# Reordering the entry of an eight-core diffusion trunk: load order, split modulation, squares summed on TensorE, a chunked first matmul group

## The chip, the cores and the metric

The kernel runs on all eight cores of one Trainium2 chip, each with its own share of the tokens and the whole set of weights. The metric is the device time of the slowest core in microseconds (us). Some executions fall into a slower state, in which the cores of one die show a lower granted clock; only executions of the fast state are compared here.

## The reference, cut to what matters

Two trunk layers work on tokens of width 1024. Each sub-layer norms its input and modulates it with a scale and a shift that come from a small product of the condition vector; each layer is two half-step SwiGLU FFNs around a mixer.

```python
def modulate(x, g, shift, scale):
    return rms_norm(x, g) * (1 + scale[:, None, :]) + shift[:, None, :]

def swiglu(h, w1, w2):
    gate, up = jnp.split(h @ w1, 2, axis=-1)
    return (jax.nn.silu(gate) * up) @ w2

for l in range(DEPTH):
    mod = jax.nn.silu(cvec) @ ada_w[l] + ada_b[l]  # (Bc, 9D)
    sh1, sc1, g1, sh2, sc2, g2, sh3, sc3, g3 = jnp.split(mod, N_MOD, axis=-1)
    x = x + 0.5 * g1[:, None, :] * swiglu(modulate(x, norm_g[l, 0], sh1, sc1),
                                          ffn_w1[l, 0], ffn_w2[l, 0])
    # ... mixer (attention and convolution in layer 0, pooling in layer 1), second FFN
```

So before the first FFN matmul a core needs: x of a tile, its sum of squares, the scale and shift of the first FFN (a quarter of a layer's `ada_w` less a bit: 8 of 36 blocks), and a block of `w1`.

## The kernel before: the parts that the change touches

A core has 1280 tokens in three tiles (512, 512, 256 columns), held transposed: 128 partitions, 8 chunks of the model width. Weights come through a ring of 16 slots; one load reads 1 MiB of float32 and lands as bf16 (the cast is GpSimd's queue's). The program is planned in Python while it is built: generators yield operations, a list scheduler gives each a start time from a small cost model, takes the earliest, and so fixes the order of every engine's instructions. **On the chip each engine follows that order, whatever really lands first** (run 2 shows it: norm steps whose inputs are ready at 67 us run at 96). The DMA model serves all loads one after another in the order of issue, at `DMA_RATE` bytes per ns.

```python
# ... Sched
    DMA_RATE = 330.0
    DMA_LAT = 1900.0
# ... xload: all of x on SyncE's queue, tile after tile, in halves
        for t, (c0, n, v) in enumerate(TILES):
            for hf in range(2):
                # ...
                yield self.dma(SP, self.xres[:, 4 * hf:4 * hf + 4, c0:c0 + n], src, [], ...)
# ... order of the ring loads (GpSimd's queue)
            yield from ada(0, 0, 8)                       # shift blocks 0-3, scale blocks 4-7
            yield from mix(w1(0, 0), ada(0, 8, 36))
            yield from w2(0, 0)
            # ... mixer weights
            yield from mix(w1(0, 1), ada(1, 0, 20))
# ... rstd: one float32 matmul with ones over the summed squares
        acc = yield from self.sumsq(t, ver, engs)         # ScalarE/GpSimd square, VectorE/GpSimd add
        yield self.mm([(ps, self.onesf[:], acc[1][:, 0:n], True, True)], ..., f32=True)
# ... norm
        yield self.wait(("asc", l, i))                    # all four scale blocks (the shifts came earlier)
        for c in range(8):
            yield self.stt(nv, self.xres[:, c, c0:c0 + n], asc[:, i, c, v:v + 1], r, ALU.mult, ALU.mult, ...)
            # ... then ScalarE adds the shift and writes hbuf[:, c]
# ... ffn: a tile is taken only when all 8 chunks of h are planned
                if j >= NJ or not self.has(("h", t, l, i), 8) or ("w1", l, s, j) not in self.W:
                    continue
```

## Time and profile before

| | before |
|---|---|
| median of 5 executions | 1657.51 us (fast ones 1654.14 to 1657.51) |
| spans of the cores, profiled execution | 1638.5 to 1652.5 us |
| TensorE busy | 88% of the span |
| first FFN matmul (mean of the eight cores) | 112.5 us |
| first FFN over, that is first product of the mixer (mean) | 369.6 us |
| mixer over, that is first matmul of the second FFN (mean) | 705.0 us |

The three stage times are read from each core's TensorE timeline: they split the span into entry, first FFN, mixer and rest. The lines themselves are in the prediction. A line of a timeline has start and duration in us, engine, line of kernel.py, operation, output<-input, shapes and count; in brackets follow the engine's idle time before it and what ended that. A line of the chain of waits has start, duration and what the kernel waited for or did. h is the normed and modulated input of an FFN (`hbuf`); a ring load is named after its weights (`adaw` for a modulation block, `w1t` for a block of w1).

### The profile page before, as it was taken

The numbers are of one execution on the slowest core, as the hardware profiler recorded it, in microseconds if no ns is written. First come the engines' busy times: TensorE is split into PE (matmuls) and PEld (weight loads), VectorE is DVE, ScalarE is ACT, GpSimd is POOL, SyncE is SP. The second block draws the span as 40 slices with busy tenths as digits, with TensorE's granted clock in tenths as the row PEclk, the third lists the DMA queues.
The fourth block names the chain that finished last, engine by engine and source line by source line (L and its number), as shares of the span: only waits on it lengthen the run. The fifth ranks groups of instructions, "written<-read, shape, count | busy, mean of one in ns | idle before, by whom it ended". The sixth has DMA issues, their size and how long they took to land.

```text
span 1652.5 us, 25909 instructions; the slowest of 8 cores (1638.5 to 1652.5 us)
## 1 busy us (share of the span) xinstructions
PE 1453.5 (88%) x9548; PEld 804.2 (49%) x9548; DVE 515.9 (31%) x936; ACT 428.6 (26%) x690; POOL 368.3 (22%) x479
## 2 busy tenths in 40 slices
PE   0039999999888786889999999999999869999997
PEld 0015555545654443445555456555544635555445
DVE  0142222135775122442222134222213574222133
ACT  1141111111303767541111014111101264111000
POOL 3111110144622010111000444110035530000244
PEclk9999999999999575799999999999999979999999
DMA  9969996300479300077434106994312273331012
GB/s 175 194 96 143 154 150 116 52 7 11 71 131 153 65 2 1 1 119 130 75 61 77 26 1 94 169 176 75 63 26 40 48 132 65 64 62 29 1 51 77
DMA packets 43068, 131.48 MB, mean 80 GB/s; under 512 B 6336, under 2 KB 10176, under 8 KB 42944
## 3 DMA queue, kind: packets, MB, share of 16 engines
q0 software_dynamic: 33440, 117.27, 43.3%
q1 hardware_dynamic: 9504, 12.54, 2.7%
q8 instruction: 79, 1.29, 0.3%
q14 instruction: 45, 0.37, 0.1%
HBM read 240.50 MB, written 6.55 MB: 150 GB/s over the span
## 4 chain that ended last, share of the span: by engine, by line
PE 74%; DMA 8%; DVE 5%; ACT 5%; issue 4%; POOL 2%; another core or an unknown queue 2%; DVEq 0%; SPq 0%; ACTq 0%; POOLq 0%
PE ps L291 74%; DMA sb_ring<-adaw 5%; DMA sb_xres<-xin 3%; DVE sb_nt L310 2%; ACT sb_sg L307 1%; ACT sb_hbuf L307 1%; ACT sb_areg L307 1%; DVE sb_areg L315 1%; POOL sb_ring L340 1%; DVE sb_xres L310 1%; DVE sb_sg L315 1%; ACT sb_rs L307 0%; DVE sb_acc L315 0%; POOL sb_acc L315 0%
## 5 line engine op out<-in xcount | busy, mean ns | idle before, releaser
L291 PE MATMUL ps<-sb_hbuf,sb_ring 128*128 128x512 bf16 (+1 forms) x4512 | 835.3, 346 | 18.6 <-ACT sb_hbuf L307 15.4
L291 PEld LDWEIGHTS ps<-sb_hbuf,sb_ring 128*128 128x128 bf16 x4512 | 438.7, 98 | 387.6 <-issue 34.3
L291 PE MATMUL ps<-sb_areg,sb_ring 128*128 128x512 bf16 (+1 forms) x2304 | 425.8, 346 | 5.0 <-DVE sb_xres L310 4.2
L315 DVE TENSOR_TENSOR sb_areg<-ps,sb_sg 128x512 bf16<-128x512 f32 (+1 forms) x264 | 159.0, 602 | 546.3 <-PE ps L291 541.1
L291 PEld LDWEIGHTS ps<-sb_areg,sb_ring 128*128 128x128 bf16 x2304 | 224.9, 98 | 201.0 <-issue 17.5
L307 ACT ACTIVATE sb_sg<-ps 128x512 f32<-128x512 f32 (+3 forms) x280 | 146.8, 525 | 660.4 <-PE ps L291 644.8
L315 POOL TENSOR_TENSOR sb_sq<-sb_xres 128x512 f32<-128x512 f32 (+1 forms) x102 | 98.3, 965 | 381.9 <-DVE sb_xres L310 222.7
L310 DVE SCALAR_TENSOR_TENSOR sb_xres<-ps,sb_gsc,sb_xres 128x512 f32<-128x512 f32 (+1 forms) x144 | 93.2, 658 | 253.0 <-PE ps L291 248.9
L315 POOL TENSOR_TENSOR sb_acc<-sb_acc,sb_sq 128x512 f32<-128x512 f32 (+1 forms) x102 | 115.8, 1136 | 17.9 <-DVE sb_acc L315 3.8
L340 POOL DMA_DIRECT2D sb_ring<-w1t x88 | 47.8, 547 | 288.1 <-PE ps L291 251.4
L310 DVE SCALAR_TENSOR_TENSOR sb_nt<-sb_xres,sb_asc,sb_rs 128x512 f32<-128x512 f32 (+1 forms) x144 | 99.1, 721 | 39.5 <-ACT sb_rs L307 24.0
L291 PE MATMUL ps<-sb_acc,sb_onesf 128*128 128x512 f32 (+1 forms) x42 | 23.4, 644 | 96.0 <-DVE sb_acc L315 53.5
L291 PE MATMUL ps<-sb_areg 64*128 64x512 bf16 (+3 forms) x728 | 87.7, 315 | 17.0 <-ACT sb_areg L307 9.1
L307 ACT ACTIVATE sb_hbuf<-sb_nt,sb_modsb 128x512 bf16<-128x512 f32 (+1 forms) x144 | 89.8, 649 | 39.6 <-DVE sb_nt L310 38.8
L340 POOL DMA_DIRECT2D sb_ring<-w2t x44 | 23.3, 529 | 271.6 <-PE ps L291 264.6
L307 ACT ACTIVATE sb_rs<-ps 128x512 f32<-128x512 f32 (+1 forms) x21 | 11.0, 524 | 263.8 <-PE ps L291 263.6
L340 POOL DMA_DIRECT2D sb_ring<-adaw x72 | 39.3, 548 | 165.8 <-PE ps L291 156.9
L307 ACT ACTIVATE sb_areg<-ps,sb_amask 128x1024 bf16<-128x1024 f32 x48 | 52.6, 1114 | 46.8 <-PE ps L291 46.6
L291 PEld LDWEIGHTS ps<-sb_areg 64*128 64x128 bf16 (+1 forms) x728 | 39.4, 109 | 49.6 <-issue 41.3
L291 PE MATMUL ps<-sb_scb,sb_ring 128*128 128x2 bf16 x1152 | 38.8, 164 | 25.5 <-DMA sb_ring<-adaw 25.5
L291 PEld LDWEIGHTS ps<-sb_scb,sb_ring 128*128 128x128 bf16 x1152 | 38.0, 98 | 44.3 <-issue 35.2
L307 ACT ACTIVATE sb_sg<-ps,sb_amask 128x1024 bf16<-128x1024 f32 x48 | 53.2, 1115 | 11.7 <-PE ps L291 11.0
(66 smaller groups left out, 459.9 us busy)
## 6 DMA issues: line engine op xcount, KB each, us to landing
sb_ring<-w1t POOLq DMA_DIRECT2D x88, 512.0 KB, 9.8
sb_ring<-adaw POOLq DMA_DIRECT2D x72, 512.0 KB, 10.7
sb_ring<-w2t POOLq DMA_DIRECT2D x44, 512.0 KB, 6.2
sb_xres<-xin SPq DMA_DIRECT2D x4, 1024.0 KB, 39.1
sb_areg<-mp POOLq DMA_DIRECT2D x5, 512.0 KB, 7.0
sb_ring<-wcx POOLq DMA_DIRECT2D x4, 512.0 KB, 10.8
sb_ring<-wo POOLq DMA_DIRECT2D x4, 512.0 KB, 26.7
yo<-sb_nt SPq DMA_DIRECT2D x8, 256.0 KB, 2.1
```

The lines of the kernel that those rows point to most:

```text
L291: ins = e.matmul(m[0], lhsT=m[1], rhs=m[2], start=m[3], stop=m[4], **({"skip_group_check": True} if len(m) > 5 else {}))
L307: return Op(ACT, lambda e: e.activation(out=out, in_=in_, func=func, **kw), reads, writes, cost)
L310: return Op(DVE, lambda e: e.scalar_tensor_tensor(out=out, in0=in0, scalar=scalar, in1=in1, op0=op0, op1=op1), reads, writes, 150.0 + 1.04 ...
L315: return Op(eng, lambda e: e.tensor_tensor(out=out, in0=in0, in1=in1, op=op), reads, writes, c)
L340: return Op(q, lambda e: e.dma_start(out=out, in_=in_), reads, writes, 600.0 if q == POOL else 450.0, True, nbytes, key)
```

## The change

Its intent is to let TensorE start on the first FFN as soon as one tile is there, by asking for less before it.

```diff
-    DMA_RATE = 330.0
+    DMA_RATE = 315.0
 # xload: SyncE's queue brings tile 0 only
+        yield from self.xtile(0, SP)
+        yield self.wait("xin")
 # order of the ring loads
-            yield from ada(0, 0, 8)
-            yield from mix(w1(0, 0), ada(0, 8, 36))
+            for i in range(4):
+                yield from ada(0, 4 + i, 5 + i)
+                yield from ada(0, i, i + 1)
+            a = list(w1(0, 0))
+            yield from a[0:6]
+            yield from mix(a[6:], ada(0, 8, 28))
 ...
+            yield from ada(0, 28, 36)                     # after the mixer's weights
             yield from mix(w1(0, 1), ada(1, 0, 20))
+            if key in (("w1", 0, 0, 2), ("w1", 0, 0, 3)): # tiles 1 and 2 of x on GpSimd's queue
+                yield from self.xtile(key[3] - 1, POOL)
+                self.sigl("xin")
 # norm: two chunks wait for their own scale and shift block
-        yield self.wait(("asc", l, i))
         for c in range(8):
+            yield self.wait(("mod", l, i, c // 2), 2)
 # entry norm: bf16 squares, summed by eight bf16 matmuls with ones
+        IN = [(ACT, True), (DVE, True)] * 4
         for t in range(3):
-            S.spawn(self.norm(t, 1, 0, 0, MX), 0)
+            S.spawn(self.norm(t, 1, 0, 0, IN), 0)
 # first group of the first FFN: w1 blocks 0 and 1, chunk by chunk over four PSUM banks
+            if (l, s) == (0, 0) and j == 0 and ("w1", l, s, 1) in self.W:
+                # ...
+                for c in range(8):
+                    yield self.wait(("h", t, l, i), c + 1)
+                    yield self.mm([(self.psv(ks[q], n), ..., self.hbuf[:, c, c0:c0 + n], c == 0, c == 7)
+                                   for q in range(4)], ...)
 # dependencies: an engine now also waits for its own earlier reads of what it overwrites
-            for x in b.r:
-                if x.eng == eng and not x.is_dma and not dma and eng != POOL and not x.strict:
-                    continue
-                deps.add(x)
+            deps.update(b.r)
```

More of the change, by code (lines that the diff above doesn't have):

```diff
@@ L48 @@
     __slots__ = ("eng", "fn", "reads", "writes", "cost", "is_dma", "nbytes", "key", "deps", "marked", "sig", "dval",
-                 "t_end", "strict")
+                 "t_end")
     def __init__(self, eng, fn, reads, writes, cost, is_dma=False, nbytes=0, key=None):
@@ L55, in __init__ @@
         self.marked = False
-        self.strict = False
         self.sig = 0
@@ L454, in build @@
         self.identb = self.sb("identb", [128, 128], BF16)
+        self.onesb = self.sb("onesb", [128, 128], BF16)
+        self.b_onesb = Buf("onesb")
         self.cvec = self.sb("cvec", [128, 8, 2])
@@ L475, in build @@
              "dummy")]
-        self.b_mod = [[B("mod%d_%d" % (l, i)) for i in range(9)] for l in range(2)]
-        self.b_asc = [[B("asc%d_%d" % (l, i)) for i in range(3)] for l in range(2)]
+        self.b_mod = [[[B("mod%d_%d_%d" % (l, i, q)) for q in range(4)] for i in range(9)] for l in range(2)]
+        self.b_asc = [[[B("asc%d_%d_%d" % (l, i, q)) for q in range(4)] for i in range(3)] for l in range(2)]
         self.b_gsc = [[B("gsc%d_%d" % (l, i)) for i in range(3)] for l in range(2)]
@@ L502, in setup @@
         S.commit(self.memset(self.onesf[:], 1.0, [self.b_onesf]))
+        S.commit(self.memset(self.onesb[:], 1.0, [self.b_onesb]))
         S.commit(self.memset(self.dummy[:], 1.0, [self.b_dummy]))
@@ L508, in setup, with xtile @@
         S.commit(self.act(self.scb[:], self.cvec[:], AF.Silu, [self.b_cvec], [self.b_scb]))
-    def xload(self):
-        off = 0
-        for t, (c0, n, v) in enumerate(TILES):
-            for hf in range(2):
-                src = self.d_x[:, off:off + 4 * n].rearrange("p (c n) -> p c n", n=n)
-                off += 4 * n
-                yield self.dma(SP, self.xres[:, 4 * hf:4 * hf + 4, c0:c0 + n], src, [],
-                               [self.bx[t][4 * hf + i] for i in range(4)], 128 * 4 * n * 4, key="x%d%d" % (t, hf))
-                for i in range(4):
-                    self.sigl(("x", t, 4 * hf + i))
+    def xtile(self, t, q):
+        c0, n, v = TILES[t]
+        off = 8 * c0
+        for hf in range(2):
+            src = self.d_x[:, off:off + 4 * n].rearrange("p (c n) -> p c n", n=n)
+            off += 4 * n
+            yield self.dma(q, self.xres[:, 4 * hf:4 * hf + 4, c0:c0 + n], src, [],
+                           [self.bx[t][4 * hf + i] for i in range(4)], 128 * 4 * n * 4, key="x%d%d" % (t, hf))
+            for i in range(4):
+                self.sigl(("x", t, 4 * hf + i))
+    def xload(self):
+        yield from self.xtile(0, SP)
+        yield self.wait("xin")
         for (tl, d, b, nb) in ((self.finalg, self.d_finalg, self.b_finalg, 4096),
@@ L568, in seq @@
         def seq():
-            yield from ada(0, 0, 8)
-            yield from mix(w1(0, 0), ada(0, 8, 36))
+            for i in range(4):
+                yield from ada(0, 4 + i, 5 + i)
[3 more added lines that the diff above has]
+            yield from mix(a[6:], ada(0, 8, 28))
             yield from w2(0, 0)
@@ L602, in ada @@
         for l in range(2):
-            for s in range(36):
+            for s in ((4, 0, 5, 1, 6, 2, 7, 3) if l == 0 else tuple(range(8))) + tuple(range(8, 36)):
                 key = ("ada", l, s)
@@ L616, in ada @@
                 i = part // 3
-                bm = self.b_mod[l][part]
+                bm = self.b_mod[l][part][s % 4]
                 yield self.tt(self.modsb[l][:, m0:m0 + 2, :], ps,
@@ L621, in ada @@
                 self.unbank(k)
-                if s % 4 == 3:
-                    lo = 8 * part
-                    if part % 3 == 0:
-                        self.sigl(("shift", l, i))
-                    elif part % 3 == 1:
-                        a = self.asc[l][:, i, :, :]
-                        ba = self.b_asc[l][i]
-                        yield self.ts(a, self.modsb[l][:, lo:lo + 8, :], 1.0, None, ALU.add, None, [bm], [ba])
-                        yield self.tt(a, a, self.normg[:, l, i, :].unsqueeze(2).broadcast_to([128, 8, 2]), ALU.mult,
-                                      [ba, self.b_normg], [ba])
-                        self.sigl(("asc", l, i))
-                    else:
-                        g = self.gsc[l][:, i, :, :]
-                        bg = self.b_gsc[l][i]
-                        if i == 1 and l == 1:
-                            yield self.tt(g, self.modsb[l][:, lo:lo + 8, :],
-                                          self.pscale[:, :].unsqueeze(2).broadcast_to([128, 8, 2]), ALU.mult,
-                                          [bm, self.b_pscale], [bg])
-                        else:
-                            yield self.ts(g, self.modsb[l][:, lo:lo + 8, :], 1.0 if i == 1 else 0.5, None, ALU.mult,
-                                          None, [bm], [bg])
-                        self.sigl(("gate", l, i))
@@ new lines, in ada @@
+                lo = m0 % 8
+                if part % 3 == 0:
+                    self.sigl(("mod", l, i, s % 4))
+                elif part % 3 == 1:
+                    a = self.asc[l][:, i, lo:lo + 2, :]
+                    ba = self.b_asc[l][i][s % 4]
+                    yield self.ts(a, self.modsb[l][:, m0:m0 + 2, :], 1.0, None, ALU.add, None, [bm], [ba])
+                    yield self.tt(a, a, self.normg[:, l, i, lo:lo + 2].unsqueeze(2).broadcast_to([128, 2, 2]), ALU.mult,
+                                  [ba, self.b_normg], [ba])
+                    self.sigl(("mod", l, i, s % 4))
+                elif s % 4 == 3:
+                    lo = 8 * part
+                    g = self.gsc[l][:, i, :, :]
+                    bg = self.b_gsc[l][i]
+                    bms = self.b_mod[l][part]
+                    if i == 1 and l == 1:
+                        yield self.tt(g, self.modsb[l][:, lo:lo + 8, :],
+                                      self.pscale[:, :].unsqueeze(2).broadcast_to([128, 8, 2]), ALU.mult,
+                                      bms + [self.b_pscale], [bg])
+                    else:
+                        yield self.ts(g, self.modsb[l][:, lo:lo + 8, :], 1.0 if i == 1 else 0.5, None, ALU.mult,
+                                      None, bms, [bg])
+                    self.sigl(("gate", l, i))
@@ L650, in prefetch, with rstd @@
                         [self.b_dummy], 1500.0)], 0)
-    def sumsq(self, t, ver, engs):
+    def rstd(self, t, ver, plan):
         c0, n, v = TILES[t]
-        acc = yield from self.take(self.accp)
-        ba, a = acc[0], acc[1][:, 0:n]
-        for d in range(8):
-            yield self.wait(("x", t, d), ver)
-            x = self.xres[:, d, c0:c0 + n]
-            bxx = self.bx[t][d]
-            e = engs[d]
-            if d == 0:
-                if e == POOL:
-                    yield self.tt(a, x, x, ALU.mult, [bxx], [ba], POOL)
-                else:
-                    yield self.act(a, x, AF.Square, [bxx], [ba])
-                continue
-            sq = yield from self.take(self.sqp)
-            bs, s = sq[0], sq[1][:, 0:n]
-            def tail(e=e, x=x, bxx=bxx, bs=bs, s=s, sq=sq, d=d):
-                if e == POOL:
-                    yield self.tt(s, x, x, ALU.mult, [bxx], [bs], POOL)
-                    yield self.tt(a, a, s, ALU.add, [ba, bs], [ba], POOL)
-                else:
-                    yield self.act(s, x, AF.Square, [bxx], [bs])
-                    yield self.tt(a, a, s, ALU.add, [ba, bs], [ba], DVE)
-                self.sqp.give(sq)
-                self.sigl(("sumd", t, ver))
-            self.S.spawn(tail(), 1)
-        yield self.wait(("sumd", t, ver), 7)
-        return acc
@@ L684, in rstd, with squares, one @@
-    def rstd(self, t, ver, engs):
-        c0, n, v = TILES[t]
-        acc = yield from self.sumsq(t, ver, engs)
-        k = yield from self.bank()
+        acc = None
+        if not all(pe for e, pe in plan):
+            acc = yield from self.take(self.accp)
+        done, got = ("sumd", t, ver), {}
+        def squares():
+            first = True
+            for d in range(8):
+                e, pe = plan[d]
+                yield self.wait(("x", t, d), ver)
+                x, bxx = self.xres[:, d, c0:c0 + n], self.bx[t][d]
+                if first and not pe:
+                    first = False
+                    yield self.square(e, acc[1][:, 0:n], x, bxx, acc[0])
+                    self.sigl(done)
+                    continue
+                sq = yield from self.take(self.sqp)
+                def one(e=e, pe=pe, x=x, bxx=bxx, sq=sq, d=d):
+                    s = sq[1].bitcast(BF16)[:, 0:n] if pe else sq[1][:, 0:n]
+                    yield self.square(e, s, x, bxx, sq[0])
+                    if pe:
+                        got[d] = sq
+                    else:
+                        a = acc[1][:, 0:n]
+                        yield self.tt(a, a, s, ALU.add, [acc[0], sq[0]], [acc[0]], POOL if e == POOL else DVE)
+                        self.sqp.give(sq)
+                        self.sigl(done)
+                self.S.spawn(one(), 1)
@@ new lines, in rstd @@
+        self.S.spawn(squares(), 0)
+        parts = ([] if acc is None else [None]) + [d for d in range(8) if plan[d][1]]
+        nacc = sum(1 for e, pe in plan if not pe)
+        k = None
+        for q, d in enumerate(parts):
+            if d is None:
+                yield self.wait(done, nacc)
+                src = acc
+            else:
+                yield Wait(lambda d=d: d in got)
+                src = got[d]
+            if k is None:
+                k = yield from self.bank()
+            lo = d is not None
+            rhs = src[1].bitcast(BF16)[:, 0:n] if lo else src[1][:, 0:n]
+            yield self.mm([(self.psv(k, n), self.onesb[:] if lo else self.onesf[:], rhs, q == 0, q == len(parts) - 1)],
+                          [src[0], self.b_onesb if lo else self.b_onesf], [self.psb[k]], f32=not lo)
+            (self.accp if d is None else self.sqp).give(src)
@@ L688, in rstd @@
         ps, pb = self.psv(k, n), self.psb[k]
-        yield self.mm([(ps, self.onesf[:], acc[1][:, 0:n], True, True)], [acc[0], self.b_onesf], [pb], f32=True)
-        self.accp.give(acc)
         rs = yield from self.take(self.rsp)
@@ L696, in rstd, with square @@
         return rs
+    def square(self, e, out, x, bx, bo):
+        if e == ACT:
+            return self.act(out, x, AF.Square, [bx], [bo])
+        return self.tt(out, x, x, ALU.mult, [bx], [bo], e)
     def norm(self, t, ver, l, i, engs, hfree=None):
@@ L703, in norm @@
             yield Wait(hfree)
-        yield self.wait(("asc", l, i))
         asc, msb = self.asc[l], self.modsb[l]
-        bm = self.b_mod[l][3 * i]
         for c in range(8):
+            yield self.wait(("mod", l, i, c // 2), 2)
+            bm = self.b_mod[l][3 * i][c // 2]
             nt = yield from self.take(self.ntp)
@@ L710, in norm, with fin @@
             yield self.stt(nv, self.xres[:, c, c0:c0 + n], asc[:, i, c, v:v + 1], r, ALU.mult, ALU.mult,
-                           [self.bx[t][c], br, self.b_asc[l][i]], [bn])
-            def fin(c=c, nt=nt, bn=bn, nv=nv):
+                           [self.bx[t][c], br, self.b_asc[l][i][c // 2]], [bn])
+            def fin(c=c, nt=nt, bn=bn, nv=nv, bm=bm):
                 yield self.act(self.hbuf[:, c, c0:c0 + n], nv, AF.Identity, [bn, bm], [self.bh[t][c]],
@@ L746, in pick @@
                 j = todo[t]
-                if j >= NJ or not self.has(("h", t, l, i), 8) or ("w1", l, s, j) not in self.W:
+                nh = self.ev.get(("h", t, l, i), 0)
+                if j >= NJ or nh < 1 or ("w1", l, s, j) not in self.W:
                     continue
-                e = max([self.W[("w1", l, s, j)][1].w.t_end] + [b.w.t_end for b in self.bh[t]] + [S.free[PE]])
+                if nh < 8 and (not ((l, s) == (0, 0)) or j > 0 or ("w1", l, s, 1) not in self.W):
+                    continue
+                e = max([self.W[("w1", l, s, j)][1].w.t_end] + [b.w.t_end for b in self.bh[t][0:nh]] + [S.free[PE]])
+                if nh < 8:
+                    e += 2000.0
                 k = (e if e > S.free[PE] + 200.0 else S.free[PE], j, t)
@@ L753, in pick, with done1 @@
             return best
-        for _ in range(3 * NJ):
+        def done1(j):
+            left[j] -= 1
+            if left[j] == 0:
+                self.wfree(("w1", l, s, j))
+        while sum(todo.values()) < 3 * NJ:
             yield Wait(lambda: pick() is not None)
             t, j = pick()
+            c0, n, v = TILES[t]
+            if (l, s) == (0, 0) and j == 0 and ("w1", l, s, 1) in self.W:
+                todo[t] += 2
+                ks = []
+                for q in range(4):
+                    k = yield from self.bank()
+                    ks.append(k)
+                Wv = [self.W[("w1", l, s, q)] for q in range(2)]
+                for c in range(8):
+                    yield self.wait(("h", t, l, i), c + 1)
+                    yield self.mm([(self.psv(ks[q], n), Wv[q // 2][0][:, c, 128 * (q % 2):128 * (q % 2) + 128],
+                                    self.hbuf[:, c, c0:c0 + n], c == 0, c == 7) for q in range(4)],
+                                  [Wv[0][1], Wv[1][1], self.bh[t][c]], [self.psb[k] for k in ks])
+                for q in range(2):
+                    done1(q)
+                    S.spawn(evac(ks[2 * q], ks[2 * q + 1], t, q, n), 1)
+                continue
             todo[t] += 1
-            c0, n, v = TILES[t]
             Wv, bW, _i = self.W[("w1", l, s, j)]
@@ L767, in ffn @@
                            for c in range(8)], rd, [self.psb[ku]])
-            left[j] -= 1
-            if left[j] == 0:
-                self.wfree(("w1", l, s, j))
+            done1(j)
             S.spawn(evac(kg, ku, t, j, n), 1)
@@ L807, in main @@
         S = self.S
-        P8, A8 = [POOL] * 8, [ACT] * 8
-        MX = [ACT, POOL, ACT, ACT, POOL, ACT, ACT, ACT]
+        P8 = [(POOL, False)] * 8
+        MX = [(ACT, False), (POOL, False), (ACT, False), (ACT, False), (POOL, False), (ACT, False), (ACT, False), (ACT, False)]
+        IN = [(ACT, True), (DVE, True)] * 4
         for t in range(3):
-            S.spawn(self.norm(t, 1, 0, 0, MX), 0)
+            S.spawn(self.norm(t, 1, 0, 0, IN), 0)
         S.spawn(self.mixer0(), 3)
@@ L973, in qkv_tile @@
             cos = rt[:, 0, i, :].unsqueeze(1).broadcast_to([128, 10, 64])
-            sw = self.tt(v4(Bv), v4(A)[:, :, ::-1, :], sin.rearrange("p h (r f s) -> p h r f s", f=2, s=16), ALU.mult,
+            yield self.tt(v4(Bv), v4(A)[:, :, ::-1, :], sin.rearrange("p h (r f s) -> p h r f s", f=2, s=16), ALU.mult,
                          [bA, brt], [bB])
-            sw.strict = True
-            yield sw
             yield self.tt(v3(A), v3(A), cos, ALU.mult, [bA, brt], [bA])
```

## The prediction

> **What bounds the kernel now.** I read the cores first: all eight lie between 1638.5 and 1652.5 us at a granted clock of 0.948 to 0.951, so the profile is of the fast state. Then the page's row of slices: each slice is 41.3 us, the TensorE row is 0 0 3 and then 9 nearly to the end, while the DMA row is 9 9 6.
>
> ```profile
> PE   0039999999888786889999999999999869999997
> DMA  9969996300479300077434106994312273331012
> ```
>
> So TensorE is the bound from about 113 us on, and before that the core is filling itself from HBM. The chain of waits says the same: nothing of TensorE carries it before 95 us, and then one unbroken piece of 257 us.
>
> ```profile
> 3.44 46.46 DMA sb_xres<-xin
> 51.15 1.28 ACT L307
> 55.19 8.59 another core or an unknown queue
> 68.12 8.91 another core or an unknown queue
> 79.99 11.36 another core or an unknown queue
> 95.25 2.47 PE ps L291 x50
> 112.84 257.07 PE ps L291 x1716
> ```
>
> The timeline of the first 120 us shows why it takes so long:
>
> ```profile
> 12.06 0.56 PE L291 MATMUL ps<-sb_scb,sb_ring 128*128 128x2 bf16 x16 [12.06 <-DMA sb_ring<-adaw]
> ...
> 16.62 0.56 PE L291 MATMUL ps<-sb_scb,sb_ring 128*128 128x2 bf16 x16 [4.00 <-DMA sb_ring<-adaw]
> 20.09 0.63 ACT L307 ACTIVATE sb_acc<-sb_xres 128x512 f32<-128x512 f32 x1 [15.77 <-DMA sb_xres<-xin]
> ...
> 34.80 0.63 ACT L307 ACTIVATE sb_sq<-sb_xres 128x512 f32<-128x512 f32 x1 [12.04 <-DMA sb_xres<-xin]
> ...
> 91.55 0.60 POOL L315 TENSOR_TENSOR sb_sq<-sb_xres 128x256 f32<-128x256 f32 x1 [12.18 <-DMA sb_xres<-xin]
> ...
> 95.25 1.19 PE L291 MATMUL ps<-sb_acc,sb_onesf 128*128 128x256 f32 x2 [23.59 <-DVE sb_acc L315]
> ...
> 96.23 2.32 PE L291 MATMUL ps<-sb_scb,sb_ring 128*128 128x2 bf16 x80
> ...
> 98.71 1.41 DVE L310 SCALAR_TENSOR_TENSOR sb_nt<-sb_xres,sb_asc,sb_rs 128x512 f32<-128x512 f32 x2 [0.18 <-DVE sb_asc L315]
> ...
> 112.84 8.23 PE L291 MATMUL ps<-sb_hbuf,sb_ring 128*128 128x512 bf16 x24 [14.29 <-ACT sb_hbuf L307]
> ```
>
> Tile 0 of x is complete at 34.8, and its sum of squares is done by 40. But the last five modulation products (80 matmuls at 96.23) stand behind the matmul of tile 2's sum of squares in TensorE's order, and tile 2's last half lands only at 91.5. Without all eight scale and shift products no norm may start (98.71). Tiles 0 and 1 are then normed in turns, so the first FFN matmul comes 14 us later still. Nothing of those 113 us is work of the FFN.
>
> Four stretches for supply and slack (last columns: granted clock, DMA share, GB/s as written), and the pace of full TensorE work:
>
> ```profile
> 20.00:40.00 20.00, 0.33 (x1) 0.36 (x2) 3.63 (x6) 3.67 (x6) 5.13 (x5) 1.00 1.02 202
> ...
> 140.00:160.00 20.00, 20.00 (x152) 11.27 (x151) 3.87 (x9) 3.75 (x7) 2.64 (x5) 1.00 1.01 162
> ```
> ```profile
> 560.00:580.00 20.00, 16.29 (x152) 8.43 (x150) 1.44 (x6) 16.28 (x16) 0.00 (x0) 0.50 0.12 23
> 580.00:600.00 20.00, 16.98 (x128) 8.08 (x128) 3.46 (x10) 11.86 (x12) 0.00 (x0) 0.59 0.00 1
> ```
> ```profile
> 331.91 1.04 POOL L315 TENSOR_TENSOR sb_sq<-sb_xres 128x512 f32<-128x512 f32 x1 [2.31 <-DVE sb_xres L310]
> ...
> 336.66 1.04 POOL L315 TENSOR_TENSOR sb_sq<-sb_xres 128x512 f32<-128x512 f32 x1 [2.30 <-DVE sb_xres L310]
> ```
>
> A ring load reads 1 MiB of float32 (1.05 MB) and writes half of it as bf16. At 162 GB/s written, ring loads alone read 324 GB/s: 3.24 us each. GpSimd takes up a new output of the second FFN product every 4.75 us (331.91 to 336.66), which is 22 matmuls of 512 columns: 216 ns each.
>
> **What the Trainium skill says.** "DMA: Bandwidth & Descriptors", section "Queues, rings and completion order": each DMA engine goes round-robin between the queues that have work, packet by packet. The trace agrees: x on SyncE's queue moves one half of tile 0 (1.05 MB) from 20.1 to 34.8, 71 GB/s, and of the 202 GB/s written 131 are left for the ring, read at 262. So x and the early weights share one pipe, and x gets the small share. "HBM Reference", section "Specifications (TRN2)": about 358 GB/s per core with both cores of a pair streaming. Here 71 + 262 = 333 and 324, so a little lower; I use the measured rates and take it that bytes in front of the first FFN matmul decide, not the number of queues. "TensorE: Matmul & The Clock Gate", "Part 1": the array is at half clock until it was busy for some 3.4 us, and falls back after an idle window. The trace: the first FFN piece after a long idle time has 24 matmuls in 8.23 us (343 ns), later 216. "VectorE: DVE Perf Modes", section "The DRAIN you can't avoid": a semaphore after each VectorE copy cost nothing extra in its measurement. On that and on the few writes concerned I put the added same-engine waits at about zero; no view of the kernel before isolates them.
>
> **The change part by part.**
> Order of loads: SyncE loads tile 0 only. GpSimd's queue carries the eight modulation blocks as scale and shift in turns, w1 blocks 0 and 1, tile 1 of x, w1 block 2, tile 2, then w1 3, 4, 5. Needed ahead of the first FFN matmul: tile 0 (2 MiB) and ring loads 1 to 10. Loads 1 and 2 land at 12.06 and 16.62 as before; then 4.0 us each (1.05 MB at 262 GB/s) while x shares the pipe, so load 6 at 32.7; from 34.8 on 3.24 each with a little of the old rate: 7 at 36.3, 8 at 39.7, 9 at 43, 10 at 46.3. I take 47 for the start.
>
> Norm of tile 0: squares are written as bf16 by ScalarE and VectorE in turns and summed by TensorE; the second half at 34.8 plus about 3 us, a table load (1.28) and two activations (0.6 each) give the factor at 40 to 41; eight norm steps at 0.87 us (98.71 to 105.6 are eight) end at 48. The first FFN group goes chunk by chunk over four banks (32 matmuls, 6.9 us at 216 ns), so it runs beside the norm and w1 block 1 is what it waits for: 47, not 112.8. That removes 66 us.
>
> What is lost again: tile 1 lands at 46.3 + 6.5 = 53, factor at about 58, norm 59 to 66; w1 block 2 at 56, tile 2 at 60. TensorE from 47 to 66 has tile 0's group (6.9), its block 2 (3.45) and tile 1's group (6.9), 17.3 of 19 us; with coarse static ordering and a second cold start (some 15 to 20 matmuls at twice 216 ns, 3 to 4 us) I count 5 us lost. Afterwards a w1 block is 32 x 0.216 + 16 x 0.109 (estimate, half of 216 and rounding) = 8.65 us, with 1.25 modulation blocks (0.54 each) 9.3 us, against a supply of 2.25 loads x 3.24 = 7.3 us. TensorE stays the bound, less amply than before.
>
> TensorE work: bf16 sums of squares of tiles 1 and 2 now lie in the busy part, 8 x 0.216 + 8 x 0.109 = +2.6 us. Eight modulation blocks leave the first FFN, 8 x 0.54 = -4.3 us, and come back after the mixer's weights: +4.3, and up to 1 us of wait each (ten later waits for such blocks sum to 9.4 us, 25.5 less 12.1 and 4.0). DMA is idle at 560 to 600 and TensorE has gaps there, so 8 x 3.24 = 26 us of later loads only eat slack; I put this at +6 in all. The model's DMA rate of 315 for 330 is nearer the measured 324 and errs to the safe side: -2.
>
> Sum: -66 + 5 + 2.6 - 4.3 + 6 - 2 = -59, from 1657.5 to 1599.
>
> **Rivals.** (1) DMA takes TensorE's place: the early FFN runs at the pace of the loads. For it: share 1.01 at 140 to 160 already, and the earlier start has 66 us less prefetch. If the rate with x on the ring falls below 260 GB/s, stalls reach some 20 us: 1615 to 1620. Against it: 7.3 against 9.3 us per block. (2) In-order blocking returns in a new place: a product put early in TensorE's static order waits for tile 1's or 2's squares, as the 23.59 us before the matmul at 95.25 did. Tile 1 now comes in the same queue in front of the work behind it, so I expect few us; if it happens, first FFN matmul at 55 to 65, total 1610 to 1618. (3) The start is gained and given back in the mixer, because the moved blocks hold TensorE there and ring slots are scarce (16): 1610 to 1620. (4) The start does not matter because the end is set elsewhere: the unbroken TensorE piece from 112.84 speaks against it; it would give 1650.
>
> **Range and chances.** The start gain of 58 to 66 rests on measured landings; the three ways of giving some back are each worth 10 to 20 us and will hardly come together. Predicted 1599 us, 8 in 10 for 1584 to 1620. Faster by over 2% means under 1624: chance 0.93; within 2%: 0.06; slower: 0.01.
>
> **What would show it.** First FFN matmul at 45 to 50 us, waiting last for w1 block 1 or a norm step; TensorE idle under 8 us between there and 70; hardly any wait for loads from 70 to the first FFN's end; that end and every later stage 55 to 62 us earlier; eight more modulation products between about 430 and 600 us with under 1 us of wait each; span about 1593. The prediction is wrong if the first FFN matmul comes after 60, if the DMA share is 1.0 with gaps in TensorE at 70 to 200, or if the mixer grows by over 10 us.

## The result, and the profile after

Nine executions of the changed kernel have a median of 1597.04 us (fast ones 1595.61 to 1599.58), beside 1657.84 us for 17 of the kernel before. The ratio is 0.9636, with a 95% interval of 0.9626 to 0.9646. A ratio is the mean time of one kernel's fast executions over that of the other's in the same rounds, so it is not quite the quotient of the medians, which also count the slow executions.

Means of the eight cores of the profiled executions, and what each stage gained:

| stage ends with | before | after | gained in the stage |
|---|---|---|---|
| first FFN matmul | 112.5 | 47.5 | 65.0 |
| first FFN over | 369.6 | 314.8 | -10.2 |
| mixer over | 705.0 | 649.1 | 1.2 |
| end of the span | 1646.5 | 1590.2 | 0.3 |

These means differ by 56 us and the medians by 61: the profiled execution of before was the fastest of its 17 (1654.14 us, 3.7 under the median), that of the changed kernel took 1598.09, 1.1 over its median.

First the slices of the changed kernel's slowest core (core 4): TensorE's 9s begin in the third slice instead of the fourth, and the DMA row is full for five slices instead of two and a dip.

```profile
PE   1699999997988878899999999999999589999997
DMA  9999953004996100585333019983321444331012
```

The chain of waits of that core: the long waits for x and the idle stretches have made way for one wait for w1.

```profile
2.34 4.87 POOL sb_ring L336 x9
7.22 41.77 DMA sb_ring<-w1t
49.23 10.45 PE ps L287 x37
...
88.86 217.70 PE ps L287 x1448
```

And its timeline. Tile 0's second half is there at 31.85, the first FFN matmul at 49.23 waits last for a w1 block, tile 1's first half is there at 52.47. Then TensorE stands three more times:

```profile
31.85 0.69 DVE L311 TENSOR_TENSOR sb_sq<-sb_xres 128x512 bf16<-128x512 f32 x1 [10.30 <-DMA sb_xres<-xin]
...
49.23 6.74 PE L287 MATMUL ps<-sb_hbuf,sb_ring 128*128 128x512 bf16 x20 [8.20 <-DMA sb_ring<-w1t]
...
52.47 0.63 ACT L303 ACTIVATE sb_sq<-sb_xres 128x512 bf16<-128x512 f32 x1 [5.62 <-DMA sb_xres<-xin]
...
62.58 0.59 PE L287 MATMUL ps<-sb_sq,sb_onesb 128*128 128x512 bf16 x2 [2.69 <-ACT sb_sq L303]
...
69.74 0.27 PE L287 MATMUL ps<-sb_sq,sb_onesb 128*128 128x256 bf16 x1 [2.90 <-ACT sb_sq L303]
...
88.86 5.38 PE L287 MATMUL ps<-sb_hbuf,sb_ring 128*128 128x256 bf16 x40 [2.23 <-ACT sb_sg L303]
```

Read the brackets: two of the three waits are for a square made by ScalarE, one for an eviction by ScalarE (it reads a finished product from PSUM, TensorE's output memory, and applies Silu). Between 59 and 87 us ScalarE loads function tables five times (at 59.54, 63.25, 66.19, 78.20 and 86.71), because Silu of the FFN and the logarithm of the norms take turns. How full its time is between 60 and 80 us is shown by the stretch (busy us of TensorE, its weight loads, VectorE, ScalarE and GpSimd, each with its number of instructions, then granted clock, DMA share and GB/s):

```profile
60.00:80.00 20.00, 14.43 (x62) 6.40 (x63) 10.19 (x17) 16.13 (x26) 0.00 (x0) 0.91 1.03 170
```

### The profile page after: what moved, and what is told of

It reads as the page before. It is cut to its first block, busy times and chain, and to the rows that moved or that the text cites. A ratio compares the mean times of both kernels' runs of the same rounds, so it can differ in the third digit from the quotient of the medians.

```text
span 1596.5 us, 25905 instructions; the slowest of 8 cores (1584.6 to 1596.5 us)
## 1 busy us (share of the span) xinstructions
PE 1456.0 (91%) x9566; PEld 804.8 (50%) x9566; DVE 516.2 (32%) x970; ACT 429.2 (27%) x688; POOL 357.9 (22%) x471
## 4 chain that ended last, share of the span: by engine, by line
PE 79%; DMA 6%; ACT 5%; DVE 5%; issue 3%; POOL 1%; DVEq 0%; ACTq 0%; POOLq 0%; SPq 0%
PE ps L287 78%; DMA sb_ring<-adaw 3%; DMA sb_ring<-w1t 3%; DVE sb_nt L306 2%; ACT sb_sg L303 2%; ACT sb_hbuf L303 1%; ACT sb_areg L303 1%; DVE sb_areg L311 1%; POOL sb_ring L336 1%; DVE sb_sg L311 1%; DVE sb_xres L306 0%; ACT sb_rs L303 0%; PE ps L296 0%; ACT L303 0%; POOL sb_sg L311 0%
## 5 line engine op out<-in xcount | busy, mean ns | idle before, releaser
L287 PEld LDWEIGHTS ps<-sb_areg,sb_ring 128*128 128x128 bf16 x2304 | 225.0, 98 | 200.3 <-issue 16.1
L303 ACT ACTIVATE sb_sg<-ps 128x512 f32<-128x512 f32 (+2 forms) x278 | 145.5, 525 | 632.9 <-PE ps L287 622.6
L311 POOL TENSOR_TENSOR sb_sq<-sb_xres 128x512 f32<-128x512 f32 (+1 forms) x96 | 92.9, 969 | 298.6 <-DVE sb_xres L306 270.6
L306 DVE SCALAR_TENSOR_TENSOR sb_nt<-sb_xres,sb_asc,sb_rs 128x512 f32<-128x512 f32 (+1 forms) x144 | 97.8, 717 | 47.7 <-ACT sb_rs L303 31.8
L311 POOL TENSOR_TENSOR sb_acc<-sb_acc,sb_sq 128x512 f32<-128x512 f32 (+1 forms) x96 | 109.6, 1143 | 13.4 <-POOL sb_sq L311 0.9
L336 POOL DMA_DIRECT2D sb_ring<-w1t x88 | 47.5, 552 | 265.5 <-PE ps L287 264.0
L287 PE MATMUL ps<-sb_sq,sb_onesb 128*128 128x512 bf16 (+1 forms) x24 | 8.4, 426 | 36.4 <-ACT sb_sq L303 18.6
```

The lines of the kernel that those rows point to most:

```text
L287: ins = e.matmul(m[0], lhsT=m[1], rhs=m[2], start=m[3], stop=m[4], **({"skip_group_check": True} if len(m) > 5 else {}))
L303: return Op(ACT, lambda e: e.activation(out=out, in_=in_, func=func, **kw), reads, writes, cost)
L306: return Op(DVE, lambda e: e.scalar_tensor_tensor(out=out, in0=in0, scalar=scalar, in1=in1, op0=op0, op1=op1), reads, writes, 150.0 + 1.04 ...
L311: return Op(eng, lambda e: e.tensor_tensor(out=out, in0=in0, in1=in1, op=op), reads, writes, c)
L336: return Op(q, lambda e: e.dma_start(out=out, in_=in_), reads, writes, 600.0 if q == POOL else 450.0, True, nbytes, key)
```

## The experiments

All twelve kernels gave correct results. Times are medians of the fast executions; "before" is the kernel before in the same rounds on the same chip (medians of the fast ones 1655.19, 1653.19 and 1653.58 us for runs 1 to 4, 5 to 8 and 9 to 12). Stage times are means of the eight cores of one profiled execution. Run 9 is the changed kernel again, and tells how far they scatter: its stages end 0.7, 0.7 and 2.2 us earlier than in the table above, so stage differences of 1 to 2 us show nothing. In the rounds of runs 5 to 8 the changed kernel itself did not run, so differences of a few us between these runs and it may be due to the chip.

| run | us | ratio to before | first FFN matmul | first FFN over | mixer over |
|---|---|---|---|---|---|
| 1 x on SyncE, early | 1641.1 | 0.9909 | 93.1 | 357.0 | 692.3 |
| 2 x on SyncE, same order | 1628.7 | 0.9841 | 50.1 | 347.4 | 681.6 |
| 3 four blocks ahead | 1612.6 | 0.9742 | 61.1 | 327.3 | 665.0 |
| 4 old squares | 1597.7 | 0.9647 | 47.1 | 311.0 | 648.3 |
| 5 load order alone | 1600.0 | 0.9684 | 54.9 | 315.5 | 650.6 |
| 6 no chunked group | 1601.8 | 0.9693 | 46.8 | 315.4 | 651.7 |
| 7 blocks back | 1607.1 | 0.9722 | 47.7 | 318.3 | 656.9 |
| 8 squares on GpSimd | 1601.3 | 0.9687 | 47.7 | 316.3 | 651.7 |
| 9 changed kernel again | 1596.5 | 0.9654 | 46.8 | 314.1 | 646.9 |
| 10 w1 early | 1610.6 | 0.9738 | 43.9 | 324.8 | 661.8 |
| 11 rate 330 | 1595.9 | 0.9648 | 46.8 | 311.5 | 645.3 |
| 12 old waits | 1597.4 | 0.9659 | 46.8 | 314.2 | 649.3 |

The theory (A): where x is loaded, and in what order of TensorE's work that puts its sums, makes the gain. Rivals: only the shared pipe matters (B); the finer waits and the chunked group make it (C).

**Run 1: x on SyncE again, all of it early.**

```diff
-        yield from self.xtile(0, SP)
-        yield self.wait("xin")
+        for t in range(3):
+            yield from self.xtile(t, SP)
 ...
-                yield from self.xtile(key[3] - 1, POOL)
```

> The changed kernel with tiles 1 and 2 of x back on SyncE's queue right behind tile 0, as before the change; all else stays. Theory A (what stands in front in TensorE's fixed order decides, because the order is planned from a model in which x comes early): the sums of tiles 1 and 2 stand ahead of five or more modulation products again, tile 2 lands at about 91 us, the first FFN matmul comes at 95 to 100 us and the kernel takes 1630 to 1645. Rival B (only the shared pipe matters: x takes its 71 GB/s and the ring loads come 4.0 instead of 3.24 us apart): first FFN matmul at about 50, 1605 to 1618. Rival C (the gain came from the finer waits and the chunked first group, not from where x is loaded): within 5 us of 1597.

It took 1641.1 us, in theory A's range, and the first FFN matmul came at 93.1, 2 us before it; both are well outside those of B and C. What is left of the gain is 0.9% (ratio 0.9909). TensorE's timeline on its slowest core:

```profile
76.25 0.61 PE L287 MATMUL ps<-sb_scb,sb_ring 128*128 128x2 bf16 x16
89.05 0.59 PE L287 MATMUL ps<-sb_sq,sb_onesb 128*128 128x256 bf16 x2 [12.19 <-ACT sb_sq L303]
...
91.75 1.89 PE L287 MATMUL ps<-sb_scb,sb_ring 128*128 128x2 bf16 x64
93.87 8.55 PE L287 MATMUL ps<-sb_hbuf,sb_ring 128*128 128x512 bf16 x31 [0.24 <-issue]
```

Four modulation products (64 matmuls, 1.89 us) stand behind the sum of tile 2 as in the kernel before, and wait for no load when their turn comes. The DMA model serves x first, because it was issued first; the queues on the chip do not (tile 2's last half is there only at 88 us, on this core).

**Run 2: the other queue, the same order.** Tiles 1 and 2 go out at the same point of the plan, on SyncE's queue instead of GpSimd's. A comparison of the built programs showed the instructions of TensorE, VectorE and ScalarE to be the same, line for line, apart from the semaphores that they wait for.

```diff
-                yield from self.xtile(key[3] - 1, POOL)
+                yield from self.xtile(key[3] - 1, SP)
```

> Tiles 1 and 2 of x on SyncE's queue, but handed out at the same point of the plan, so that TensorE's order is the same, instruction for instruction, as in the changed kernel; only the queue differs. Theory A and B together: first FFN matmul at 48 to 52 us (tile 0 and the ring loads hardly change), tile 1 complete at about 64 and tile 2 at 91 to 96 by the round robin; TensorE then stands before the last sum of tile 2 (done at 77 in the changed kernel) until about 94: 17 us more, 1608 to 1620. If the queue does not matter: 1597 within 4 us. If it matters as much as in the kernel of the first run: over 1628.

It took 1628.7: the queue alone costs 32 us, more than the 11 to 23 that I expected, and just at the bound of my third case (over 1628). The first FFN matmul is where I had put it (50.1). From its timeline (core 2):

```profile
96.12 0.42 ACT L303 ACTIVATE sb_sq<-sb_xres 128x256 bf16<-128x256 f32 x1 [28.97 <-DMA sb_xres<-xin]
...
96.47 1.41 DVE L306 SCALAR_TENSOR_TENSOR sb_nt<-sb_xres,sb_asc,sb_rs 128x512 f32<-128x512 f32 x2
...
102.36 0.42 ACT L303 ACTIVATE sb_sq<-sb_xres 128x256 bf16<-128x256 f32 x1 [0.97 <-DMA sb_xres<-xin]
...
107.60 7.93 PE L287 MATMUL ps<-sb_hbuf,sb_ring 128*128 128x512 bf16 x36
```

The step at 107.60 is at 77.44 in the changed kernel's trace: 30 us, which is the loss. I had counted only TensorE's wait for tile 2. But VectorE and ScalarE follow a fixed order too, and the norm steps of tile 1 (96.47), whose factor had been ready since 67, stand behind tile 2's first squares. A late transfer holds all that was planned behind it on every engine, not only its own users.

**Run 3: four blocks that are needed later, ahead of w1.**

```diff
+            yield from ada(0, 8, 12)
             a = list(w1(0, 0))
 ...
-            yield from mix(a[6:], ada(0, 8, 28))
+            yield from mix(a[6:], ada(0, 12, 28))
```

> Four modulation blocks (4 MiB that are needed only later) are loaded ahead of w1 block 0; nothing is added, they only move forward. If the bytes in front of the first FFN matmul decide its start: 4 loads at 3.24 us = 13 us later, first FFN matmul at 60 to 62 us, and since TensorE is the bound afterwards the kernel takes 1607 to 1612. If the start is set by the norm or by something that does not wait for loads: within 3 us of 1597.

The first FFN matmul moved by 13.6 us (61.1 against 47.5), 3.4 for each load; the first FFN ended 12.5 later, the kernel took 16 us longer (1612.6 from two fast executions, just over the range). So the bytes in front of the first FFN matmul set its start, as the prediction had it; the last 3 us were lost in the mixer.

**Run 4: the old float32 sums.**

```diff
-        IN = [(ACT, True), (DVE, True)] * 4
+        IN = MX
```

> The changed kernel with the sums of squares at the entry made as before (ScalarE and GpSimd square, VectorE and GpSimd add in float32, one float32 matmul for each tile) in place of bf16 squares that TensorE sums. Tile 0 is complete at 32 us and w1 block 1 lands at 47 to 49, so the old sums (factor some 4 us after the tile) are in time: first FFN matmul unchanged at 47 to 50. If the squares on TensorE earn something: 1600 to 1606. If they cost something, because eight small matmuls of each tile stand between FFN matmuls and wait for ScalarE: 1588 to 1595. I expect 1592 to 1602.

1597.7, the same as the changed kernel within noise. The first FFN even ends 3.8 us earlier (3.1 against run 9), and the mixer takes it back (337.3 us instead of 334.3; 332.9 in run 9). The bf16 squares and their matmuls earn nothing here.

**Run 5: the order of loads alone**, put into the kernel before (the diff is the load part of the change: `xtile`, the order of `ada` and `w1`, the blocks behind the mixer's weights).

> The kernel before with only the order of its loads changed (scale and shift blocks in turns, tiles 1 and 2 of x on GpSimd's queue behind w1 blocks 1 and 2, the last eight modulation blocks of layer 0 after the mixer's weights). The old float32 sums, the wait for all modulation blocks, the unchunked first group, the rate of 330 and the old same-engine waits stay. Theory A (the order of the loads, and of TensorE's work that follows from it, is the gain): all eight blocks are there by 42 us, eight norm steps end at 49 to 50, first FFN matmul at 49 to 52 instead of 47.5, first FFN over (first product of the next layer part) at 312 to 319, 1594 to 1604 in all. Rival C (the finer waits and the chunked group make the gain): first FFN matmul at 60 or later, over 1615.

1600.0 and a ratio of 0.9684: of the 3.5% that the changed kernel gains in the rounds of run 9 (1 - 0.9654), the order of loads alone gives 3.2%, in other rounds. My numbers for its start were 49 to 52; it was 54.9 (on core 5 the last seven modulation products stand behind tile 0's sum and run at 42.13, so the norm begins at 46.53). Yet the first FFN ends only 0.7 us later than in the changed kernel. Its TensorE timeline (core 5) shows why:

```profile
54.70 12.11 PE L291 MATMUL ps<-sb_hbuf,sb_ring 128*128 128x512 bf16 x48 [9.40 <-ACT sb_hbuf L307]
66.65 1.02 PE L291 MATMUL ps<-sb_acc,sb_onesf 128*128 128x512 f32 x2
67.51 5.34 PE L291 MATMUL ps<-sb_hbuf,sb_ring 128*128 128x512 bf16 x24
```

It starts late but then does 72 FFN matmuls by 73 us without a pause; the changed kernel's core 4, started at 49, has done as many at 77, its other cores at 74 to 75. On the mean of the eight cores that is 73.9 here and 75.1 there. Between 47 and 90 us TensorE is not yet the bound, so its start matters less than what it stands for afterwards.

**Run 6: no chunked group.**

```diff
-                if nh < 8 and (not ((l, s) == (0, 0)) or j > 0 or ("w1", l, s, 1) not in self.W):
+                if nh < 8:
 ...
-            if (l, s) == (0, 0) and j == 0 and ("w1", l, s, 1) in self.W:
+            if False:
```

> The changed kernel without the chunked first group over four banks: a tile's first FFN matmul waits for all eight norm steps. Tile 0 is normed by 46 to 47 us and w1 block 1 lands at 47 to 49, so its start moves by 0 to 1 us; for tile 1 the group starts some 5 us later, but TensorE then has little else. Theory A: 1597 to 1603. Rival C: over 1608.

1601.8, in theory A's range and far from C's. The first FFN ends 0.6 us later than in the changed kernel; the other few us appear in the mixer and behind it. The control ran in other rounds, so whether the group itself is worth these 4 to 5 us stays open.

**Run 7: the eight modulation blocks back in the first FFN.**

```diff
-            yield from mix(a[6:], ada(0, 8, 28))
+            yield from mix(a[6:], ada(0, 8, 36))
 ...
-            yield from ada(0, 28, 36)
```

> The eight modulation blocks of layer 0 that moved behind the mixer's weights go back among the loads of the first FFN. My sum had -4.3 us in the first FFN and +6 in the mixer for the move. If that is right: first FFN ends 4 to 5 us later (319 instead of 314.8, mean of the cores), the mixer is 5 to 6 us shorter, 1594 to 1599. If the move costs nothing in the mixer (TensorE has gaps there): first FFN ends 4 to 5 later, the mixer as long as before, 1600 to 1603. If the loads of the first FFN become the bound with them: over 1605.

1607.1. That is the time of my third case, but not its cause: after its start the first FFN waits for no load (cores 0, 2, 4 and 6). It ends 3.5 us later, about the work moved (my 4.3). But the mixer is not shorter: it takes 338.5 us, 4.2 more than in the changed kernel. Here are TensorE's waits for modulation blocks from 310 to 700 us on core 6 (total us, times, longest), with the blocks back, then as changed:

```profile
PE ps L287 <- DMA sb_ring<-adaw: 8.9, 3, 6.3
```
```profile
PE ps L287 <- DMA sb_ring<-adaw: 2.2, 3, 1.0
```

With the blocks back, the mixer waits longer for blocks of layer 1, on seven of the eight cores: 8.9 to 12.7 us, against 1.2 to 4.5 in the changed kernel. The eighth (core 0) waits 1.9 us, and its mixer takes 334.6, where the seven take 337.8 to 340.6. So the waits go with the longer mixer.

**Run 8: squares of tiles 1 and 2 on GpSimd.** This was meant to remove the two waits on ScalarE at 62.58 and 69.74.

```diff
-            S.spawn(self.norm(t, 1, 0, 0, IN), 0)
+            S.spawn(self.norm(t, 1, 0, 0, IN if t == 0 else [(POOL, True), (DVE, True)] * 4), 0)
```

> The squares of tiles 1 and 2 at the entry go to GpSimd (idle at 40 to 100 us) and VectorE in turns, not to ScalarE and VectorE; the sums stay on TensorE. In the changed kernel TensorE stands twice for some 2.8 us between 60 and 70 us for a square that waits on ScalarE behind table loads and evictions. If those two waits are what the start still loses: both go, first FFN ends at 309 to 311 (314.8 now), 1590 to 1595. If GpSimd's slower squares (1.04 us for 128x512, against 0.63) or VectorE's order replace them: within 3 us of 1597.

It missed: 1601.3, outside both cases, first FFN over 1.5 us later. TensorE's waits between 47 and 100 us (core 1) include these:

```profile
PE ps L287 <- DVE sb_sq L311: 2.6, 2, 2.4
PE ps L287 <- ACT sb_sg L303: 2.4, 1, 2.4
PE ps L287 <- POOL sb_sq L311: 2.2, 3, 1.2
```

That is 7.2 us. The same core of the changed kernel waits 4.1 us for ScalarE's squares, 2.2 for its eviction and 0.8 for VectorE's squares, 7.1 in all. The waits moved to VectorE and GpSimd; they did not go.

**Run 9: the changed kernel again**, as the control of the last three.

> The changed kernel itself, on the same chip and in the same rounds as the next three, as their control: 1597 within 3 us. The mean of the cores' spans was 1590.2, first FFN over at 314.8.

1596.5, ratio 0.9654 (0.9639 to 0.9669).

**Run 10: an attempt at a faster one.** w1 blocks 0 and 1 come right behind the first pair of modulation blocks, with the old sums of run 4.

```diff
+            a = list(w1(0, 0))
             for i in range(4):
                 yield from ada(0, 4 + i, 5 + i)
                 yield from ada(0, i, i + 1)
-            a = list(w1(0, 0))
-            yield from a[0:6]
+                if i == 0:
+                    yield from a[0:2]
+            yield from a[2:6]
 ...
-        IN = [(ACT, True), (DVE, True)] * 4
+        IN = MX
```

> A version meant to beat the changed kernel: the float32 sums of the fourth run (which ended the first FFN 3.8 us earlier), and w1 blocks 0 and 1 loaded right behind the first pair of modulation blocks, so that the chunked group starts while the other three pairs still land. The first FFN matmul should come at 38 to 41 us, the group end at 48 to 50 with the last pair (54 to 57 in the changed kernel), the first FFN end at 305 to 308 and the kernel take 1588 to 1593. If what it wins is only waiting in another place, because no byte less is loaded before tile 1 can be normed: first FFN over at 310 to 312 and 1594 to 1598. If half clock in a thinly fed TensorE eats it: group end at 52 or later.

1610.6, 14 us slower than its control and outside both times that I gave; only the sign of the third case came (group end after 52). TensorE does start earlier (43.9), but its timeline (core 4) shows a loop:

```profile
52.74 1.04 PE L287 MATMUL ps<-sb_scb,sb_ring 128*128 128x2 bf16 x32
53.46 0.16 DVE L311 TENSOR_TENSOR sb_modsb<-ps,sb_adab 128x4 f32<-128x4 f32 x1 [3.28 <-PE ps L287]
...
54.77 1.42 DVE L306 SCALAR_TENSOR_TENSOR sb_nt<-sb_xres,sb_asc,sb_rs 128x512 f32<-128x512 f32 x2
55.62 1.38 ACT L303 ACTIVATE sb_hbuf<-sb_nt,sb_modsb 128x512 bf16<-128x512 f32 x2 [4.62 <-DVE sb_nt L306]
56.48 3.57 PE L287 MATMUL ps<-sb_hbuf,sb_ring 128*128 128x512 bf16 x8 [2.70 <-ACT sb_hbuf L303]
```

The next modulation product stands behind the FFN chunks of the pair before in TensorE's order, those wait for ScalarE, which waits for VectorE, which waits for the modulation product before. One turn takes 7.1 us (the next product is at 59.85), and the products wait for the turn, not for their weights. The group's last piece begins at 63.16; in the changed kernel's trace it begins at 57.57. TensorE in small portions also ran slower: the 8 matmuls at 56.48 took 3.57 us, 446 ns each instead of 216, and the granted clock is 0.67 at 60 to 80 us, 0.91 in the changed kernel. How much of the 14 us is the loop and how much the clock is not shown. No version here beats the changed kernel by more than the noise.

**Run 11: planned with the rate of 330.**

```diff
-    DMA_RATE = 315.0
+    DMA_RATE = 330.0
```

> The changed kernel planned with the old DMA rate of 330. My sum gave the new rate -2 us, by fewer waits of TensorE for modulation blocks planned too early. If that is right: 1598 to 1601, with more wait for such blocks. If the rate does nothing but reshuffle: within 3 us of the control either way.

1595.9, the same as the control: a reshuffle. TensorE's wait for modulation blocks in the whole span is 10.4 us against 7.7, on different cores; the first FFN ends 2.5 us earlier and the mixer gives some back.

**Run 12: without the added same-engine waits** (the old exception for reads by the same engine, and the one strict place, restored).

> The changed kernel without the added waits of an engine on its own earlier reads (the one strict place of before is kept). I put their cost at about zero: within 1.5 us of the control. If each one drains VectorE or ScalarE: 3 to 8 us faster than the control.

1597.4 against 1596.5: nothing. This agrees with "VectorE: DVE Perf Modes", section "The DRAIN you can't avoid", which the prediction named.

## Why the prediction was right

It said 1599 (1584 to 1620), and 1597 was measured, but not by the same sum. The signs that it named came: TensorE stands for 4.1 to 6.4 us between its start and 70 us (under 8 predicted), and the later stages end 54.8 to 56.3 us earlier (55 to 62 predicted, so at its low edge).

- **Start of the first FFN (-66): right.** 65.0 us measured. The start comes at 46.7 to 49.2 on the eight cores (predicted 47), on six of them after a wait for w1, on core 6 for h and on core 2 without a wait. So norm and loads come out almost together: in run 6, which waits for the whole norm, the start is 46.8. Run 3 shows that 3.4 us of start follow from each load in front (3.24 predicted).
- **Why it was late before: right.** Run 1 brings back the products behind tile 2's sum, and with them 46 us of start and 44 us of time. Run 2 shows that with the order unchanged the queue alone costs 32 of those 44. One reading was loose: of the five products at 96.23 only three belong to the eight that the norm waits for (its last scale step is at 98.35, after the third).
- **Lost after the start (+5, and +2.6 - 4.3 for work added and moved): too small.** These terms sum to 3.3; 10.2 us were given back by the first FFN's end. This is the term that was mis-sized. Of the +5, 1.7 were idle time; TensorE in fact stands for 7.2 to 8.7 us between its start and 100 us on the eight cores. On core 4 that is its three waits, 7.8 us, on ScalarE, which I had not looked at as a bound: it squares, evicts, writes h and swaps tables between 60 and 80 us, where it is busy for 16.1 of 20. The bf16 squares are only a part of it: the first FFN is longer than before by 10.2 us with them, still by about 7 with the old sums (run 4) and by 11.5 with GpSimd's squares (run 8). No run separates the rest.
- **Moved blocks (-4.3 and +6): half right.** The first FFN gained 3.5 (run 7), but the mixer lost nothing by the move: it takes 334.3 us, against 335.5 before and 338.5 with the blocks back. The +6 was wrong.
- **The rate (-2) and the waits (0):** nothing in either case (runs 11 and 12). The reason given for the rate was wrong too: 330 is 6 away from the measured 324, 315 is 9.
- **Rivals.** DMA did not take TensorE's place for longer: the share is 1.0 from 40 to 180 us, but on the slowest core TensorE has no gap from 100 to 300 us. In-order blocking was the real danger (runs 1, 2 and 10); of it the changed kernel has only the short waits named above. Nothing was given back in the mixer.

So the start was understood, and the rest of the sum came out by luck: a loss that was put too small by 7 us met later terms that were put too large by 5 to 6 (+6 - 2 = +4 predicted, -1.5 measured in the mixer and behind it). And the sum of -59 lies between the 56 us of the profiled executions and the 61 of the medians, so it can't be judged more closely than that.

## What to carry to other kernels

In a kernel whose engines follow an order fixed at build time, check the planned arrival of every early load against the real one, queue by queue: one transfer that comes later than planned holds all the work behind it, on every engine it touches. Put what the first useful work needs in front on one queue, in the order in which it is used, and count the bytes ahead of it. Breaking a wait into small pieces can cost time where the pieces form a loop through several engines (run 10); an early start is worth little where the later steps are not ready (run 5).

## What the Trainium skill lacked or had wrong

- "DMA: Bandwidth & Descriptors", "Queues, rings and completion order": it tells of the round robin but not what share a queue gets. Here x in 2 KB rows beside ring loads had 71 of 333 GB/s, and in run 2 the same bytes on the other queue cost 32 us.
- "ScalarE: Activation LUTs", "What ACT_TABLE_LOAD costs": it gives about 1283 ns for the load and 1380 ns for a drain, 2.66 us for every switch. The load agrees (1283 ns is the mean of the 22 on core 4 of the changed kernel), but no drain shows: there the load at 66.19 begins 0.02 us after the activation before it ends, and the next activation begins 0.01 us after the load.
- "TensorE: Matmul & The Clock Gate", "Part 1": it says to budget a clock of 13/16 when all cores run dense matmuls. In the fast state the granted clock was 1.00 from 100 to 300 us with TensorE busy throughout, and 22 matmuls of 512 columns took 4.75 us (216 ns each, kernel before); a share near 13/16 (0.81) was seen only in slow executions, as the mean of a slow core over its span (0.831 to 0.838 in one of the changed kernel, 0.795 to 0.808 in one of run 3).
- No page has it: the granted clock in this profile does not show every slow stretch. The first 20 FFN matmuls of the changed kernel took 6.74 us (337 ns each) in a stretch listed at 1.00, while run 10's slow matmuls lie in stretches listed at 0.79 and 0.67.
